# One product of 512 columns written as four of 128 in the recurrence of an RWKV-7 / forgetting-attention trunk

## The chip, the core and the metric

The kernel runs on one core of a Trainium2 chip. TensorE (PE) does matrix products, and the loading of its stationary operand is shown as an engine of its own (PEld). VectorE (DVE), ScalarE (ACT) and GpSimd (POOL) do the elementwise work, and SyncE (SP) issues most DMA transfers. The metric is the device time of one execution in microseconds (us). Before the change it is 2595.79 us, the median of three runs (2594.67 to 2596.96).

## The reference, cut to what matters

Two layers work on 256 tokens of width 2048 in float32: RWKV-7 time mixing with a SwiGLU, then forgetting attention with a SwiGLU. The change is in the first. Each of 32 heads of width 64 carries a 64x64 state through the tokens:

```python
def step(S, inp):
    r_t, w_t, k_t, v_t, a_t, b_t = inp
    sa = jnp.einsum('bhij,bhj->bhi', S, a_t)
    S = (S * w_t[:, :, None, :] + sa[..., None] * b_t[:, :, None, :]
         + v_t[..., None] * k_t[:, :, None, :])
    return S, jnp.einsum('bhij,bhj->bhi', S, r_t)
...
w_log = -jax.nn.softplus(-(w0 + jnp.tanh(xw @ w1) @ w2).astype(f32)) - 0.5
decay = jnp.exp(-jnp.exp(w_log))
```

The kernel does not step token by token. It works on chunks of 64 tokens and needs, for every token and channel, the product of the decays from the chunk's start, which is the exponential of a running sum of log decays.

## The kernel before, in words

**The weight stream.** Every large product runs in `Stream.gemm`: weights arrive by DMA in 128x1024 pieces (`st`), ACT rounds each 128x512 block to a high half (`wh`, L147), DVE subtracts to get the low half (`wl`, L148), and PE multiplies in three products of 512 columns each (L180 to L182). They are called large products here. They follow each other through the whole kernel.

**Background work.** After each group of three, `tick` lets up to eight generators go one step. They issue everything else, PE's small products included, so small products lie between the large ones in one queue on PE. The builder then places the instructions of every engine by its own estimate of when each is ready, so the final order differs in details from that of the code. Each engine executes its queue in order.

**The recurrence.** It is cut into eight units, one for each of four groups of eight heads and two halves of 128 tokens. For each unit four generators follow each other:
- `prepare` (L579) makes the decays and scaled keys. Its first product (L587) multiplies a constant 128x128 triangular matrix (two blocks of 64 tokens) with `tw`, the log decays of the unit: 128 tokens by 512 channels. The result fills one PSUM bank. DVE (L599) and two ACT exponentials (L600, L601) read the whole of it. Transposes (L642, L655, L669) and head products (L681, masked by DVE in L684) follow.
- `solve` (L695) copies diagonal blocks (L708, ACT) and inverts 8x8 triangles on DVE (L713 to L733).
- `merge` (L736) joins them with small 32x32 products (L758, L765, L775, L791), each run of which waits for DVE or ACT results (`Ti`, `Xs`).
- `chain` (L809) carries the state through the unit's two chunks (L838, L842, L848, L854, L856).
- `post` normalises the output, and transposes it (L911).

PE reads float32 operands of these small products as they are. In the trace such a product has two records of MATMUL and two of LDWEIGHTS, a transpose has one of each, and a large product, whose operands are rounded halves, one of each. The last unit's running sums are made at 489 us; the rest of the kernel, to 2597 us, has no instruction of the recurrence after about 590 us.

## Time and profile before

| | |
|---|---|
| median of 3 runs | 2595.79 us (2594.67 to 2596.96) |
| the profiled execution's own time | 2598.75 us |
| its span, first to last instruction | 2597.0 us |
| PE busy | 2549.0 us, 98% |
| DVE / ACT busy | 1694.3 us (65%) / 1409.5 us (54%) |
| chain that ended last, PE's share | 89% |
| the changed line, 8 products | 16 MATMUL records of 9.3 us in all |

Records on PE overlap: a record lasts from the product's start to its modelled end, and the next product starts before that. What a product costs is therefore read from the distance of starts, not from its duration. An idle time in square brackets at a row's end is time in which PE had nothing running, with what ended it.

### The profile page before, as it was taken

The numbers are of one execution on the slowest core, as the hardware profiler recorded it, in microseconds if no ns is written. First come the engines' busy times: TensorE is split into PE (matmuls) and PEld (weight loads), VectorE is DVE, ScalarE is ACT, GpSimd is POOL, SyncE is SP. The second block draws the span as 40 slices with busy tenths as digits, with TensorE's granted clock in tenths as the row PEclk, the third lists the DMA queues.
The fourth block names the chain that finished last, engine by engine and source line by source line (L and its number), as shares of the span: only waits on it lengthen the run. The fifth ranks groups of instructions, "written<-read, shape, count | busy, mean of one in ns | idle before, by whom it ended". The sixth has DMA issues, their size and how long they took to land.

```text
span 2597.0 us, 40783 instructions
## 1 busy us (share of the span) xinstructions
PE 2549.0 (98%) x15104; PEld 2081.7 (80%) x15104; DVE 1694.3 (65%) x3049; ACT 1409.5 (54%) x2605; POOL 90.1 (3%) x73
## 2 busy tenths in 40 slices
PE   7999999999999999999999999999999999999998
PEld 5788777778888888888888888888888888888887
DVE  7886999987555555555556777676655555555554
ACT  6665666556455544545545656555655545454444
POOL 0000011100000000000001011010000000000000
PEclk9999999999999999999999999999999999999999
DMA  6667434345565565555556666664565655565554
GB/s 193 183 201 241 135 102 115 110 140 186 188 193 187 189 192 186 192 189 188 193 191 204 191 210 181 187 203 152 190 194 186 189 189 189 187 193 188 194 195 162
DMA packets 271222, 472.66 MB, mean 182 GB/s; under 512 B 39464, under 2 KB 49976, under 8 KB 271024
## 3 DMA queue, kind: packets, MB, share of 16 engines
q1 hardware_dynamic: 267728, 467.33, 56.6%
q10 hardware_dynamic: 3136, 2.74, 0.3%
q8 instruction: 118, 1.93, 0.3%
q14 instruction: 80, 0.66, 0.1%
q0 software_dynamic: 160, 0.00, 0.0%
HBM read 459.47 MB, written 6.32 MB: 179 GB/s over the span
## 4 chain that ended last, share of the span: by engine, by line
PE 89%; DVE 5%; ACT 3%; DMA 2%; issue 1%; POOL 0%; SPq 0%; POOLq 0%; ACTq 0%; DVEq 0%
PE mm L180 27%; PE mm L181 27%; PE mm L182 27%; DVE wl L148 2%; ACT wh L147 1%; DMA st<-in_a_w_rkv_dram 1%; PE bg L1012 1%; PE bg L856 1%; PE bg L310 1%; PE bg L1248 0%; PE bg L838 0%; PE bg L848 0%; PE bg L462 0%; PE bg L854 0%; DMA x<-in_x_dram 0%
## 5 line engine op out<-in xcount | busy, mean ns | idle before, releaser
L148 DVE TENSOR_TENSOR wl<-st,wh 128x512 fp32r<-128x512 f32 (+1 forms) x1648 | 1128.1, 690 | 795.2 <-ACT wh L147 790.1
L147 ACT CAST wh<-st 128x512 fp32r<-128x512 f32 (+1 forms) x1648 | 1017.0, 622 | 980.0 <-DVE wl L148 688.5
L180 PE MATMUL mm<-wh,xb 128*128 128x512 f32 x2048 | 803.5, 392 | 0.0
L182 PE MATMUL mm<-wh,xb 128*128 128x512 f32 x2048 | 799.7, 390 | 0.0
L181 PE MATMUL mm<-wl,xb 128*128 128x512 f32 x2048 | 799.4, 390 | 0.0
L180 PEld LDWEIGHTS mm<-wh,xb 128*128 128x128 f32 x2048 | 384.7, 188 | 79.8 <-issue 3.3
L182 PEld LDWEIGHTS mm<-wh,xb 128*128 128x128 f32 x2048 | 384.5, 188 | 79.4
L181 PEld LDWEIGHTS mm<-wl,xb 128*128 128x128 f32 x2048 | 384.8, 188 | 75.8
L180 PE MATMUL mm<-wh,xa 128*128 128x512 f32 x768 | 310.3, 405 | 0.0
L181 PE MATMUL mm<-wl,xa 128*128 128x512 f32 x768 | 304.9, 397 | 1.5 <-DVE wl L148 1.5
L182 PE MATMUL mm<-wh,xa 128*128 128x512 f32 x768 | 304.3, 397 | 0.0
L180 PE MATMUL mm<-wh,hb 128*128 128x512 f32 x448 | 174.3, 389 | 0.0
L181 PE MATMUL mm<-wl,hb 128*128 128x512 f32 x448 | 174.3, 389 | 0.0
L182 PE MATMUL mm<-wh,hb 128*128 128x512 f32 x448 | 174.3, 389 | 0.0
L181 PEld LDWEIGHTS mm<-wl,xa 128*128 128x128 f32 x768 | 145.7, 190 | 30.8 <-DVE wl L148 3.2
L180 PEld LDWEIGHTS mm<-wh,xa 128*128 128x128 f32 x768 | 145.5, 190 | 31.0 <-issue 1.7
L182 PEld LDWEIGHTS mm<-wh,xa 128*128 128x128 f32 x768 | 145.2, 189 | 30.3
L181 PEld LDWEIGHTS mm<-wl,hb 128*128 128x128 f32 x448 | 84.1, 188 | 17.5
L180 PEld LDWEIGHTS mm<-wh,hb 128*128 128x128 f32 x448 | 84.1, 188 | 17.4
L182 PEld LDWEIGHTS mm<-wh,hb 128*128 128x128 f32 x448 | 84.1, 188 | 17.4
L1196 POOL TENSOR_TENSOR n<-n,pw 128x8 f32<-128x8 f32 x24 | 45.1, 1882 | 411.7 <-DVE n L1195 411.7
L1239 ACT ACTIVATE sc<-sc,nm 128x128 f32<-128x128 f32 x64 | 28.7, 449 | 26.6 <-DVE nm L1238 26.6
(294 smaller groups left out, 1826.2 us busy)
## 6 DMA issues: line engine op xcount, KB each, us to landing
st<-in_f_w_gu_dram SPq DMA_DIRECT2D x352, 512.0 KB
st<-in_f_w_d_dram SPq DMA_DIRECT2D x176, 512.0 KB
st<-in_b_w_in_dram SPq DMA_DIRECT2D x128, 512.0 KB
st<-in_a_w_rkv_dram SPq DMA_DIRECT2D x96, 512.0 KB
st<-in_a_w_o_dram SPq DMA_DIRECT2D x32, 512.0 KB
st<-in_b_w_o_dram SPq DMA_DIRECT2D x32, 512.0 KB
cb<-cdram SPq DMA_DIRECT2D x4, 1024.0 KB
x<-in_x_dram SPq DMA_DIRECT2D x12, 256.0 KB
```

Source lines behind the costliest of these rows:

```text
L147: nc.scalar.copy(hi[:rows, :n], st)
L148: nc.vector.tensor_tensor(lo[:rows, :n], st, hi[:rows, :n].bitcast(F32), op=ALU.subtract)
L180: nc.tensor.matmul(ps[t][:, :n], xh[:rows, c], wh, start=b == 0, stop=False)
L181: nc.tensor.matmul(ps[t][:, :n], xh[:rows, c], wl, start=False, stop=False)
L182: nc.tensor.matmul(ps[t][:, :n], xl[:rows, c], wh, start=False, stop=b == kts - 1)
L310: nc.tensor.transpose(tp[:, i * T + t * P : i * T + (t + 1) * P], src[:, t, c : c + P], ident)
L856: mm(pb[half[1 - q], ps_], M[:, q * 8 + s_, 0:C], vu[:, hs], start=first, stop=first or p == 3)
L1012: nc.tensor.transpose(tp[:, j * P : (j + 1) * P], h[:, j * P : (j + 1) * P], ident)
L1196: nc.gpsimd.tensor_tensor(n8[:, :], n8[:, :], pw[:, :], op=ALU.pow)
L1239: nc.scalar.activation(sc[:, c], sc[:, c], AF.Exp, bias=nm[:, t : t + 1], accum_out=nm[:, 2 + t : 3 + t])
```

## The change

The one product of 512 columns becomes four of 128 columns with the same stationary matrix. Each writes its quarter of the same PSUM bank, each with `start` and `stop` set. Nothing else is edited.

```diff
                     ps = yield from S.take()
-                    mm(ps[:, :], cst[:, C_TRI : C_TRI + P], tw[:, :], start=True, stop=True)
+                    for p in range(4):
+                        mm(ps[:, p * P : (p + 1) * P], cst[:, C_TRI : C_TRI + P], tw[:, p * P : (p + 1) * P], start=True, stop=True)
                     kk = u1.tile([P, 512], F32, name="kk")
                     nc.vector.tensor_tensor(kk[:, :], k, vk[:, :], op=ALU.mult)
```

The file gains a line, so lines from L588 on have a number that is one higher after the change (L758 becomes L759). Because the builder places instructions by its estimates, some others move too. On PE, at the first unit, the product stands where it stood. Before:

```order
L182 MATMUL mm<-wh,xa_1479 128x512
L587 MATMUL bg<-tw_2799,cst 128x512
L180 MATMUL mm<-wh,xa_1478 128x512
L181 MATMUL mm<-wl,xa_1478 128x512
L182 MATMUL mm<-wh,xa_1479 128x512
```

and after:

```order
L182 MATMUL mm<-wh,xa_1479 128x512
L588 MATMUL bg<-tw_2799,cst 128x128 x4
L180 MATMUL mm<-wh,xa_1478 128x512
L181 MATMUL mm<-wl,xa_1478 128x512
L182 MATMUL mm<-wh,xa_1479 128x512
```

Nothing moved here: four products stand in the place of one. The first difference in order on PE is behind the second unit's sums, at the first unit's merge (some 295 us into the span); `mm` are large products, `bg` small ones. Before:

```order
L180 MATMUL mm<-wh,xa_1478 128x512
L181 MATMUL mm<-wl,xa_1478 128x512
L758 MATMUL bg<-Ti,El 32x32 x32
L182 MATMUL mm<-wh,xa_1479 128x512
L180 MATMUL mm<-wh,xa_1478 128x512
L181 MATMUL mm<-wl,xa_1478 128x512
L765 MATMUL bg<-Xs,Tt 32x32 x32
L182 MATMUL mm<-wh,xa_1479 128x512
```

and after:

```order
L180 MATMUL mm<-wh,xa_1478 128x512
L759 MATMUL bg<-Ti,El 32x32 x32
L181 MATMUL mm<-wl,xa_1478 128x512
L182 MATMUL mm<-wh,xa_1479 128x512
L180 MATMUL mm<-wh,xa_1478 128x512
L766 MATMUL bg<-Xs,Tt 32x32 x32
L181 MATMUL mm<-wl,xa_1478 128x512
L182 MATMUL mm<-wh,xa_1479 128x512
```

Both runs of 32 small products stand one large product earlier, with three large products between them as before. The same happens in most places of the recurrence from here on where the order differs; in a few a run stands one later, and the five runs of the chain product L848 whose place differs go both ways. All 9888 large products stay, and the order is the same again behind the last unit.

On DVE, between the second unit's masks (L684) and its sums' first reader (L599), one instruction changes places with two. Before:

```order
L684 TENSOR_TENSOR xb_2580<-bg,cst 128x512 x2
L626 TENSOR_REDUCE bon<-rr 128x8
L684 TENSOR_TENSOR xb_2580<-bg,cst 128x512 x2
L631 TENSOR_TENSOR kk<-kk,n_3090 128x512
L148 TENSOR_TENSOR wl<-st,wh 97x512
L599 TENSOR_TENSOR WW<-bg,tw_2802 128x512
```

and after:

```order
L685 TENSOR_TENSOR xb_2580<-bg,cst 128x512 x2
L627 TENSOR_REDUCE bon<-rr 128x8
L632 TENSOR_TENSOR kk<-kk,n_3096 128x512
L685 TENSOR_TENSOR xb_2580<-bg,cst 128x512 x2
L148 TENSOR_TENSOR wl<-st,wh 97x512
L600 TENSOR_TENSOR WW<-bg,tw_2802 128x512
```

The scaling of the keys (`kk`) went ahead of the second pair of masks; what stands behind the two is unchanged up to the first unit's merge.

## Rows read from the trace of the kernel before

**Rows 1.** The page: busy time of each engine, and the share of each engine in the chain of work that ended last.

```profile
PE 2549.0 (98%) x15104; PEld 2081.7 (80%) x15104; DVE 1694.3 (65%) x3049; ACT 1409.5 (54%) x2605; POOL 90.1 (3%) x73
...
PE 89%; DVE 5%; ACT 3%; DMA 2%; issue 1%; POOL 0%; SPq 0%; POOLq 0%; ACTq 0%; DVEq 0%
```

**Rows 2.** Busy time by stage: before the recurrence, the recurrence, and the rest. [...]

```profile
0.00:256.00 256.00, 233.02 (x1088) 190.91 (x1089) 198.45 (x412) 154.43 (x317) 5.48 (x11) 0.99 0.66 204
256.00:584.00 328.00, 311.84 (x4789) 238.53 (x4788) 296.52 (x673) 202.40 (x425) 33.57 (x28) 0.99 0.41 122
584.00:2597.00 2013.00, 2004.10 (x9231) 1652.26 (x9229) 1199.36 (x1966) 1052.71 (x1863) 51.09 (x34) 1.00 0.59 189
```

**Rows 3.** The line that changes, L587: durations in ns (least, median, most), first and last start, shape; then what its readers waited for it (us, times).

```profile
L587 PEld LDWEIGHTS bg<-tw,cst x16: 186/188/189, 260.2 to 488.7; 128*128 128x128 f32 x16
L587 PE MATMUL bg<-tw,cst x16: 590/592/1061, 260.4 to 489.2; 128*128 128x512 f32 x16
...
  DVE WW L599: 0.4, 1
```

**Rows 4.** PE in order of time around the second of the eight products (start us, duration us, instruction).

```profile
281.27 1.02 PE L587 MATMUL bg<-tw,cst 128*128 128x512 f32 x2
281.72 0.80 PE L180 MATMUL mm<-wh,xa 128*128 128x512 f32 x1
282.36 0.40 PE L181 MATMUL mm<-wl,xa 128*128 128x512 f32 x1
282.59 0.39 PE L182 MATMUL mm<-wh,xa 128*128 128x512 f32 x1
```

**Rows 5.** PE in order of time where float32 products of 64 columns, each with a new 128x128 stationary operand, follow each other (in the attention layer).

```profile
1463.95 0.39 PE L1256 MATMUL bg<-v,pT 128*128 128x64 f32 x2
1464.17 0.39 PE L1257 MATMUL bg<-v,pT 128*128 128x64 f32 x2
1464.40 0.39 PE L1255 MATMUL bg<-v,pT 128*128 128x64 f32 x2
```

**Rows 6.** PE in order of time around eight transposes of 128 columns, each with a 128x128 stationary operand.

```profile
474.76 1.09 PE L655 MATMUL bg<-cst,WW 128*128 128x128 f32 x8
475.61 0.71 PE L182 MATMUL mm<-wh,xa 128*128 128x512 f32 x2
476.16 0.40 PE L180 MATMUL mm<-wh,xa 128*128 128x512 f32 x1
476.40 0.39 PE L181 MATMUL mm<-wl,xa 128*128 128x512 f32 x1
```

**Rows 7.** In order of time, PE and DVE around the longest idle time of PE in the recurrence, the first unit's merge.

```profile
294.67 0.39 PE L181 MATMUL mm<-wl,xa 128*128 128x512 f32 x1
...
298.04 0.63 DVE L732 STREAM_TRANSPOSE Ti<-Xb 128x256 f32<-128x256 f32 x1
...
298.77 1.07 PE L758 MATMUL bg<-Ti,El 32*32 32x32 f32 x64 [3.72 <-issue]
```

**Rows 8.** Stretches of 2 us from there on, and one later in the recurrence; columns as in rows 2.

```profile
296.00:298.00 2.00, 0.00 (x0) 0.00 (x0) 1.95 (x5) 0.14 (x1) 0.14 (x1) 1.00 0.00 0
298.00:300.00 2.00, 1.23 (x65) 1.19 (x66) 2.00 (x6) 0.11 (x1) 0.22 (x1) 0.71 0.00 0
300.00:302.00 2.00, 2.00 (x51) 1.25 (x55) 1.98 (x4) 0.85 (x2) 0.00 (x0) 0.50 0.42 100
302.00:304.00 2.00, 2.00 (x98) 1.50 (x92) 1.47 (x5) 0.66 (x2) 0.00 (x0) 0.94 0.70 238
...
408.00:410.00 2.00, 2.00 (x24) 0.60 (x25) 2.00 (x4) 1.93 (x5) 0.00 (x0) 0.52 0.53 202
```

**Rows 9.** PE in order of time at three more idle times in the recurrence.

```profile
399.40 0.52 PE L758 MATMUL bg<-Ti,El 32*32 32x32 f32 x37 [0.69 <-DVE Ti L767]
...
451.37 0.68 PE L848 MATMUL bg<-u,TT 64*64 64x64 f32 x16 [0.77 <-ACT u L846]
...
515.12 0.38 PE L758 MATMUL bg<-Ti,El 32*32 32x32 f32 x21 [2.02 <-issue]
```

**Rows 10.** What PE waited for most between 258 and 600 us (who, for whom; us in total, times, longest).

```profile
PE bg L758 <- issue: 6.0, 3, 3.7
PE bg L848 <- ACT u L846: 3.8, 5, 1.2
PE bg L765 <- issue: 1.7, 3, 1.0
PE bg L758 <- DVE Ti L767: 1.5, 3, 0.7
PE bg L669 <- DVE xb L659: 1.1, 4, 0.4
```

**Rows 11.** DVE and ACT in order of time between the second unit's masks and sums.

```profile
282.21 1.27 DVE L684 TENSOR_TENSOR xb<-bg,cst 128x512 f32<-128x512 f32 x2
283.40 0.68 DVE L631 TENSOR_TENSOR kk<-kk,n 128x512 f32<-128x512 f32 x1
...
283.87 1.23 ACT L708 COPY Dg<-xb 32x256 f32<-32x256 f32 x3
...
285.20 0.41 DVE L713 TENSOR_TENSOR Xb<-Dg,cst 128x256 f32<-128x256 f32 x1
```

## The prediction

> **What bounds the kernel now.** I read the page's busy times and its chain first [rows 1]. PE is busy for 98% of the span and holds 89% of the chain that ended last; DVE has 5%, ACT 3%. Next comes the table by stage [rows 2], since an average over the span hides where PE is not alone. From 584 us on PE is busy for 2004.10 of 2013 us. In the recurrence, 256 to 584 us, it is busy for 311.84 of 328 us: 16.2 us idle, while DVE is busy for 296.52 us, 90% of the stretch. So in the changed stage PE's own time is the first limit, and DVE's chains are the second. What PE waits for there is in the list of waits [rows 10]: merge products and state products, waiting for DVE and ACT. No row of that list names the changed line, and its readers waited for it once, for 0.4 us [rows 3].

> Two things can therefore change the time: what PE needs for four products in place of one, and what the changed order does to PE's idle time.

> **The products themselves.** L587 has 16 records for 8 products, so each product is two passes over its 512 columns [rows 3]. In order of time [rows 4], L587 starts at 281.27; the next large product is queued from 281.72 and the one behind it starts at 282.36. Large products follow each other in 0.23 us (282.36 to 282.59), so the queued one had its turn at 282.13. L587 thus takes 282.13 - 281.27 = 0.86 us, 0.43 a pass. That is 0.1075 us for 128 columns. Four products need eight passes of 128 columns: streamed without a gap, again 0.86 us. The low end is no change; a gain is excluded, since the same columns pass at the same pace.

> What is new is that the stationary matrix is loaded eight times per unit, not twice. The trace has no float32 product of 128 columns with a new full stationary operand, so I bound it by neighbours. With 64 columns and a new 128x128 operand [rows 5], a product starts every 0.2225 us (1463.95, 1464.17, 1464.40), 0.111 a pass. Streaming 64 columns takes 0.054, so something else sets that pace, and only the load is there. Either it runs beside the stream and takes 0.111 itself; then a pass of 128 columns takes 0.111, eight take 0.89, and a unit costs 0.03 more: 0.2 us over eight units. Or it stands in series and takes 0.111 - 0.054 = 0.057; then a pass takes 0.165, eight take 1.32, and a unit costs 0.46 more: 3.7 us. The nearest row in shape is eight transposes, of 128 columns and with 128x128 operands [rows 6]: they start at 474.76; the third large product behind them starts at 476.16, which puts the end of the eight at 476.16 - 2 x 0.23 = 475.70. That is 0.94 for eight, 0.1175 each. I take this one: 0.08 us more a unit, **0.6 us** over eight.

> [...]

> **The changed order.** The builder gives four products other estimates than one, so runs of small products move against the large ones, mostly one place ahead. At the first unit's merge, PE is idle for 3.72 us until L758 starts at 298.77, when DVE's L732 (298.04 plus 0.63) is done [rows 7]. DVE works through those microseconds without a gap [rows 8], so L732 does not come sooner or later. L758 now stands one large product earlier: PE waits 0.23 longer and runs that product afterwards, where PE has no idle time and the granted clock is 0.50 [rows 8]. That is 2 x 0.23 = 0.46 us. At 399.40 [rows 9] L758 waits for L767, which depends on L765; four large products stand between these as before, and both move together: nothing. At 451.37 [rows 9] L848 waited 0.77 for ACT and stands one large product later: 0.23 less. At 515.12 [rows 9] nothing moves. The sum is **0.2 us**. Where a moved run meets no idle time, the same work is done in another order, at no cost.

> On DVE the second pair of masks starts 0.60 later (282.81 for 282.21). The ACT copies behind them (L708) ended at 283.87 + 1.23 = 285.10 and L713 took them at 285.20 [rows 11]. Now the second mask ends near 284.1 and two copies of 0.41 end near 284.9: covered by L599, and if it were not, at most 0.6 us. On SP, some loads of the state's values change places with one weight load; PE waits for ACT and DVE in rows 10, for no DMA, so I cost that at nothing; without this cover a late piece would cost PE what it is late.

> The bounds of the order as a whole are wide. Some 27 runs stand one large product earlier; if all met idle time, it would be 27 x 0.23 = 6.2 us more. Downwards, the idle time of rows 10, 14.1 us in five rows, could in part go. The places that I could follow say 0.2, and I stay there.

> **Sum.** The profiled execution took 2598.75 us, 1.75 more than its span. 2598.75 + 0.6 + 0.2 = 2599.6. That execution is 2.96 us (0.11%) above the median of the runs, so for the median I say 2595.79 + 0.8 = **2596.6 us**. A measurement of this kernel tells a change from none at about 0.2%, here 5.2 us: 2590.6 to 2601.0 is no change.

> **Rivals.**
> - *The loads stand in series with the streams* (0.165 a pass): 3.7 + 0.2, or 2599.7 us, still no change. Were the whole 0.111 load and nothing hidden, a pass would take 0.111 + 0.1075 = 0.2185, a unit 1.75, and the kernel 7.1 us more: 2603.1 us, slower. For it: nothing in these rows hides a float32 load behind a float32 stream of 128 columns beyond doubt. Against it: rows 6 at 0.1175. [...] 5% for the smaller, 2% for the larger.
> - *A new long wait and a drop of the clock*: slower. Behind the 3.72 us of idling the granted clock was 0.71, 0.50 and 0.94 in three stretches of 2 us [rows 8], which loses 0.58 + 1.00 + 0.12 = 1.7 us. A second place like it costs 3.7 + 1.7 = 5.4, with the 0.8 above 6.2: 2602.0 us. The clock falls at a second place now, near 408 us [rows 8]; a third could be the merge at 515.12, which idles 2.02 already [rows 9]; DVE is 90% busy, so a step of solve put behind two others is late by more than one of them. It decides from about 4.4 us of added loss on. Against it: the exchanges on DVE are by one or two places. 6%.
> - *The long wait at 298.77 shrinks or another goes*: faster. If the 3.72 and the 1.7 behind it went, 0.8 - 5.4 = -4.6: 2591.2 us, short of the bound alone; with 0.77 from 451.37 it is 2590.4. Against it: L732 ends a chain of DVE that has no gap. 4%.

> **Chances and range.** The forecast holds 83%, the series rival 5% of no change, the larger 2%, the new wait 6%, the lost wait 4%. Faster 0.04, same 0.88, slower 0.08. The unknown of the order sets the range: about 3.5 us down; up by 3.7 for the series price and a little: 2593.0 to 2601.0.

> **What would show it.** L588 has 64 MATMUL and 64 LDWEIGHTS records; starts inside a group of eight lie 0.11 to 0.12 apart, where 0.165 shows the series and 0.21 the larger price. PE's idle time from 256 to 584 us stays within 3 us of 16.2; L759 still starts near 298.8 behind some 3.95 us of idling; the clock falls there and near 408 us and at no third place; the stage behind keeps its length. A recurrence that is longer by over 4 us with PE no busier would prove me wrong by the order, and one with PE busier by as much, by the loads.

## The result, and the profile after

The changed kernel takes 2600.14 us, the median of 22 runs (2594.37 to 2607.64), against 2595.82 of the kernel before (22 runs, 2594.03 to 2600.73): the ratio is 1.0015, with a 95% interval of 1.001 to 1.0021. That is no change by the bound of 0.2% and inside the range (2593.0 to 2601.0). It is also 4.3 us, clear of zero, where the forecast had 0.8. The cause of that difference is what the experiments are about.

The page of the changed kernel answers to [rows 1]; PE has 48 more records, as 64 stand for 16:

```profile
PE 2549.7 (98%) x15152; PEld 2087.4 (80%) x15152; DVE 1694.0 (65%) x3049; ACT 1410.2 (54%) x2605; POOL 89.5 (3%) x73
...
q8 instruction: 119, 1.95, 0.3%
...
PE 90%; DVE 4%; DMA 2%; ACT 2%; issue 1%; SPq 0%; POOLq 0%; POOL 0%; ACTq 0%; DVEq 0%
```

The row in the middle is from the list of DMA queues: packets, MB, share of 16 engines. 119 packets of 1.95 MB are 16 KB each; it matters below.

PE in order of time around the second unit's four products, to be read against [rows 4], and the line's durations, against [rows 3]:

```profile
277.66 0.40 PE L182 MATMUL mm<-wh,xa 128*128 128x512 f32 x1
277.90 1.05 PE L588 MATMUL bg<-tw,cst 128*128 128x128 f32 x8
278.70 0.48 PE L180 MATMUL mm<-wh,xa 128*128 128x512 f32 x1
279.02 0.39 PE L181 MATMUL mm<-wl,xa 128*128 128x512 f32 x1
...
L588 PE MATMUL bg<-tw,cst x64: 271/275/377, 257.0 to 493.5; 128*128 128x128 f32 x64
```

By the same working as before, the eight passes end where the next large product had its turn, 279.02 - 0.23 = 278.79, and took 278.79 - 277.90 = 0.89 us, 0.111 each. That fits the load running beside the stream, at the pace of [rows 5]; in series it would have been 0.165 or more. On PEld the eight loads start at 277.76 and their records last 0.99 us in all, so they lie beside the eight passes in time. One product of 512 columns took 0.86, so four cost 0.03 more a unit, 0.24 us in eight units. In five of the eight units one of the seven distances between starts is 0.213 in place of 0.111. That is not a price of the change: the kernel before has the same 0.105 more between its two passes there (0.533 for 0.428), in four of the five units, and in the fifth its product ran at the lower clock.

By stage the difference is in the recurrence. The rows are to be read against [rows 2]; the columns there and here are the stretch and its length, busy us of PE, PEld, DVE, ACT and POOL, each with its instructions, the granted clock of PE as a share of its full one, the DMA share, GB/s:

```profile
256.00:584.00 328.00, 310.65 (x4814) 242.73 (x4814) 292.71 (x667) 198.59 (x419) 32.94 (x28) 0.97 0.40 118
584.00:2598.00 2014.00, 2005.33 (x9238) 1653.83 (x9236) 1200.78 (x1968) 1054.20 (x1865) 51.08 (x34) 1.00 0.62 189
```

The granted clock over the stretch is 0.97 where it was 0.99. The two spans differ by 0.9 us only, because the profiled execution of before had lost time earlier. From 60 to 100 us its granted clock was 0.91, against 1.00 after; before and after:

```profile
60.00:100.00 40.00, 36.99 (x172) 29.99 (x172) 35.25 (x79) 24.45 (x53) 0.00 (x0) 0.91 0.61 179
```

```profile
60.00:100.00 40.00, 37.83 (x189) 30.52 (x188) 36.91 (x83) 26.89 (x59) 0.00 (x0) 1.00 0.61 186
```

That costs 40 x 0.09 = 3.6 us, ahead of the first changed instruction. So I compare the recurrence alone, from the first record of the running sums to the last of the outputs' transposes (L911, after the change L912). Before it is 585.6 - 260.4 = 325.2 us [first start in rows 3; the last start of L911 is 585.6]. After it is 587.3 - 257.0 = 330.3. The recurrence grew by 5.1 us in this pair of profiles.

Where PE stood idle in it, to be read against [rows 7] and [rows 9]:

```profile
295.38 1.08 PE L759 MATMUL bg<-Ti,El 32*32 32x32 f32 x64 [3.87 <-issue]
...
431.65 0.74 PE L759 MATMUL bg<-Ti,El 32*32 32x32 f32 x62
435.03 0.26 PE L759 MATMUL bg<-Ti,El 32*32 32x32 f32 x2 [2.65 <-issue]
...
470.01 0.65 PE L766 MATMUL bg<-Xs,Tt 32*32 32x32 f32 x52
472.04 0.31 PE L766 MATMUL bg<-Xs,Tt 32*32 32x32 f32 x12 [1.38 <-issue]
```

The first is the forecast wait, 3.87 us. The others are of another kind. A run of 32 equal products (64 records) is stopped after 62 records, or after 52, although the run had already been released. Behind both stops the granted clock falls to its lower level, 0.50:

```profile
434.00:436.00 2.00, 0.97 (x6) 0.88 (x6) 0.45 (x2) 0.37 (x1) 0.00 (x0) 0.73 0.12 33
436.00:438.00 2.00, 2.00 (x57) 1.67 (x59) 1.92 (x6) 1.16 (x3) 0.00 (x0) 0.50 0.03 8
...
472.00:474.00 2.00, 1.96 (x25) 1.17 (x26) 1.55 (x5) 0.00 (x0) 0.00 (x0) 0.62 0.65 193
474.00:476.00 2.00, 2.00 (x33) 1.74 (x30) 2.00 (x5) 1.16 (x3) 0.00 (x0) 0.50 0.78 237
476.00:478.00 2.00, 2.00 (x6) 1.39 (x5) 1.02 (x4) 1.92 (x6) 0.84 (x1) 0.50 0.28 103
478.00:480.00 2.00, 2.00 (x39) 1.51 (x38) 1.46 (x3) 1.60 (x4) 0.80 (x1) 0.68 0.00 0
```

Summed over stretches of 2 us from 250 to 592 us, (1 - clock) times the stretch is 3.4 us before and 8.5 us after; PE's idle time is 16.2 and 17.4 us. So the recurrence grew mostly by work done at the lower clock. Of the 5.1 us more, 1.7 stand at the first merge and 1.7 + 3.4 behind the two stops, and the 1.7 near 408 us of before [rows 8] are gone.

### The profile page after: what moved, and what is told of

The parts are those of the page before. It is cut to its first block, busy times and chain, and to the rows that moved or that the text cites. A ratio compares the mean times of both kernels' runs of the same rounds, so it can differ in the third digit from the quotient of the medians.

```text
span 2597.9 us, 40880 instructions
## 1 busy us (share of the span) xinstructions
PE 2549.7 (98%) x15152; PEld 2087.4 (80%) x15152; DVE 1694.0 (65%) x3049; ACT 1410.2 (54%) x2605; POOL 89.5 (3%) x73
## 3 DMA queue, kind: packets, MB, share of 16 engines
q8 instruction: 119, 1.95, 0.3%
## 4 chain that ended last, share of the span: by engine, by line
PE 90%; DVE 4%; DMA 2%; ACT 2%; issue 1%; SPq 0%; POOLq 0%; POOL 0%; ACTq 0%; DVEq 0%
PE mm L180 28%; PE mm L181 27%; PE mm L182 27%; DMA st<-in_a_w_rkv_dram 1%; DVE wl L148 1%; PE bg L1013 1%; PE bg L857 1%; PE bg L310 1%; ACT wh L147 0%; PE bg L839 0%; PE bg L1249 0%; PE bg L849 0%; PE bg L855 0%; DVE xmf L375 0%; DMA st<-in_a_w_o_dram 0%
## 5 line engine op out<-in xcount | busy, mean ns | idle before, releaser
L180 PEld LDWEIGHTS mm<-wh,hb 128*128 128x128 f32 x448 | 84.1, 188 | 17.4
L181 PEld LDWEIGHTS mm<-wl,hb 128*128 128x128 f32 x448 | 84.1, 188 | 17.4
```

The costliest lines, as they stand in the source:

```text
L180: nc.tensor.matmul(ps[t][:, :n], xh[:rows, c], wh, start=b == 0, stop=False)
L181: nc.tensor.matmul(ps[t][:, :n], xh[:rows, c], wl, start=False, stop=False)
```

## What stops a run in its middle

The kernel before has such stops as well: the run at 515.12 in [rows 9] had done 43 of 64 records. I counted the position of each stop in PE's program, with a LDWEIGHTS and a MATMUL for each record and the few instructions that only wait. In the profile of before the six stops inside a run stand at instruction 6337, 6594, 7617, 9922, 10945 and 11201; in that of after the three stand at 7617, 8897 and 9922. All nine leave 193 or 194 when divided by 256. PE has 30384 such instructions in the trace of before and 30482 in that of after, and 256 go into them 118.7 and 119.1 times: the page's queue q8, "instruction", has 118 and 119 packets of 16 KB. Its 1.93 and 1.95 MB come to 63.6 and 64.0 bytes for each of those instructions, and 16 KB over 256 to 64.

To forecast with it I worked out a count, an estimate: over all borders of the recurrence, how much less than 4.5 us the 256 instructions before a border take, by distances of starts (0.2275 us for a large product, 0.1175 for a transpose, 0.0107 for a 32x32 record, and so on). It is 15.7 us before and 19.6 after. Only its differences mean something, since its size hangs on the 4.5 us, a choice that no run measures. It stands in the expectations of the last four runs below and not in those of the first two, whose times were known by then: for these two it is no forecast.

**The packets in time.** The trace has a start and a duration for each packet of that queue, so the theory can be tested without any new run. Taken in order there is one packet for each border, from the second border on. The packet for the stop at 435.03 is alone in its queue in a stretch of a quarter of a microsecond (432.50 to 432.75 us):

```profile
q8 instruction: 1, 0.02, 23.8%
```

23.8% of 16 engines in 0.25 us is 0.95 us. By the trace it starts at 432.61, so it has landed at 433.56, and PE goes on 1.47 us later. For the stop at 472.04 it is 469.57 + 1.19 = 470.76, 1.28 us earlier. The same holds in all profiles of this case: the six stops of before, the three of after and the 13 of five runs below end 1.24 to 1.56 us after their packet has landed. None of the borders in the eight profiles, stop or not, is passed sooner than 1.24 us after its packet's landing. The packets start between 5.0 us before and 4.7 us after PE passes the border one piece earlier. So a piece that is used up faster than the next one starts, lands and is taken over ends in a stop.

The stops at borders add up to 4.4 us in the profile of before, in six, and to 4.4 us in that of after, in three. So it is not their sum that differs between these two profiles, but the time at the lower clock.

## Experiments

The ratios below are those on record, each with its 95% interval; they are not quotients of the medians.

**Borders moved, order kept.** Extra products of 8 columns at the very start, where PE waits for its input (11.3 us for the DMA of `gr` in the profile of before), write into a free part of a tile that nobody reads. Everything else on PE keeps its order.

```diff
             tp = now(S.take())
+            for _ in range(18): mm(tp[0:8, 256:264], pw[:, 0:8], pw[:, 0:8], start=True, stop=True)
             nc.tensor.transpose(tp[:, 0:112], gr[0:112, 0, :], ident[0:112, 0:112])
```

In the kernel before:

> The kernel before with 18 extra products of 8 columns (72 PE instructions) at the very start, where PE waits for its first input; their result is read by nobody, and the order of everything else on PE is that of before. Fetch theory (PE's instructions arrive in pieces of 256, and where the border between two pieces falls into a run of short products PE waits for the next piece): the borders move by 72 instructions, into denser runs, so slower than before by 3 to 6 us, 2599 to 2602 us, with idle times inside runs of the 32x32 products that are not there before. Order theory (the moved runs of small products cost the time): no change, 2595.8 within 1.5 us, since the order is that of before. Product theory (four products of 128 columns cost more than one of 512): no change, since the product is that of before.

Measured: 2598.51 us against 2596.11 of the kernel before in the runs beside it, ratio 1.0006 (0.9997 to 1.0015). The time is just under the range I gave, a miss of the fetch theory's size, and its interval includes no change, so by itself it decides nothing. Its profile does say where the borders went:

```profile
432.81 0.24 PE L759 MATMUL bg<-Ti,El 32*32 32x32 f32 x2 [1.57 <-issue]
...
470.08 0.25 PE L766 MATMUL bg<-Xs,Tt 32*32 32x32 f32 x5 [1.32 <-issue]
...
516.23 0.25 PE L766 MATMUL bg<-Xs,Tt 32*32 32x32 f32 x3 [0.62 <-issue]
```

They come behind 62, 59 and 61 of the 64 records, at instructions 7618, 8898 and 10178, which leave 194 again. In the kernel before none of the three stood there.

In the changed kernel:

> The changed kernel with the same 18 extra products of 8 columns at the start, where PE waits; the order of the rest is that of the changed kernel. Fetch theory: the borders move into sparser places than in the changed kernel, and sparser than in the kernel before, so 4 to 6 us less than the changed kernel, 2594 to 2597 us, at or below the kernel before. Order theory and product theory: as the changed kernel, 2600 us within 1.5, since order and products are the same.

Measured: 2593.93 us (2590.98 to 2597.77), ratio to the kernel before 0.9992 (0.9983 to 1.0001). This is 6.2 us less than the changed kernel takes, though PE's order and its products are unchanged and more was added. Order theory and product theory fall here. Its recurrence lasts 579.9 - 255.8 = 324.1 us, and the two places where the clock fell after the change show it undisturbed, with small stops only:

```profile
364.75 0.44 PE L760 MATMUL bg<-Ti,El 32*32 32x32 f32 x27 [0.24 <-issue]
...
432.20 0.53 PE L760 MATMUL bg<-Ti,El 32*32 32x32 f32 x38 [0.70 <-issue]
...
434.00:436.00 2.00, 1.68 (x70) 1.22 (x62) 1.90 (x5) 1.49 (x4) 0.00 (x0) 1.00 0.12 27
472.00:474.00 2.00, 2.00 (x14) 1.80 (x15) 1.65 (x5) 1.94 (x4) 1.12 (x1) 1.00 0.50 183
```

**Is it the extra work at the start that helps?** The same edit with 64 products, one whole piece, and with 50:

```diff
+            for _ in range(64): mm(tp[0:8, 256:264], pw[:, 0:8], pw[:, 0:8], start=True, stop=True)
```

> The changed kernel with 64 extra products of 8 columns at the start, 256 PE instructions: one whole piece. Fetch theory: the borders fall on the same instructions as in the changed kernel, so as slow as that, 2600 us within 2, and the idle times stand inside the same runs of 32x32 products. If instead extra products at the start help by themselves (a busier PE while it waits for its input, an earlier first stage), 64 of them help no less than 18 did: 2594 us or less.

Measured: 2599.56 us (2597.53 to 2600.89), ratio 1.0013 (1.0004 to 1.0022). A whole piece gives the changed kernel's time back, and its stops, after the same records (62 and 52):

```profile
435.48 0.26 PE L760 MATMUL bg<-Ti,El 32*32 32x32 f32 x2 [3.07 <-issue]
...
473.91 0.31 PE L767 MATMUL bg<-Xs,Tt 32*32 32x32 f32 x12 [1.06 <-issue]
```

> The changed kernel with 50 extra products of 8 columns at the start, 200 PE instructions. Fetch theory: counted over the borders, the time by which the 256 instructions before a border take less than 4.5 us is 14.3 us, as with 18 extra products (14.4) and below the changed kernel's 19.6: 2594 us within 2. If the gain grows with the number of extra products or is chance, it has no reason to come back here: 2600 us, or somewhere between.

Measured: 2594.45 us (2592.61 to 2596.91), ratio 0.9998 (0.9989 to 1.0007). So 0, 18, 50 and 64 extra products give 2600.1, 2593.9, 2594.5 and 2599.6 us: the time goes with the position within a piece, not with how much is added.

**The count without the products of 128 columns.**

```diff
                     ps = yield from S.take()
+                    for _ in range(3):
+                        mm(ps[0:8, 0:8], pw[:, 0:8], pw[:, 0:8], start=True, stop=True)
                     mm(ps[:, :], cst[:, C_TRI : C_TRI + P], tw[:, :], start=True, stop=True)
```

> The kernel before, its one product of 512 columns kept, with three extra products of 8 columns ahead of it in each unit, so that the number of PE instructions per unit is that of the changed kernel. Fetch theory: the borders move as in the changed kernel (20.8 us by the count above, 19.6 there), so 2599 to 2603 us though no product of 128 columns is there. Product theory: 2596 to 2597 us, since three products of 8 columns in eight units cost PE some 1 us.

Measured: 2600.74 us (2597.48 to 2603.39), ratio 1.0015 (1.0006 to 1.0024): the loss of the changed kernel, with its number of instructions and without its products. In its profile a unit's three small products start about 0.026 us a record apart (six records in 0.30 us, the last of 0.169), 0.16 us for the six, or 1.3 us in eight units, where the forecast of the product theory had some 1 us. The order on PE differs from both kernels here, so this run alone does not part order from borders; the runs above do. Its profile also has a fall of the clock, from 373.87 us, behind a wait for DVE that ends at 373.06 (0.99 us). This one stands at a border too, but its packet had landed 6.75 us earlier, so it is no wait for instructions.

**Two products of 256 columns.**

```diff
-                    mm(ps[:, :], cst[:, C_TRI : C_TRI + P], tw[:, :], start=True, stop=True)
+                    for p in range(2):
+                        mm(ps[:, p * 256 : (p + 1) * 256], cst[:, C_TRI : C_TRI + P], tw[:, p * 256 : (p + 1) * 256], start=True, stop=True)
```

> Two products of 256 columns in place of the four of 128: four more PE instructions per unit than before, not twelve. Fetch theory: 14.8 us by the count above, a little below the kernel before (15.7), so 2594 to 2597 us. Product theory: between the two kernels, 2597 to 2598 us, since the number of products and loads lies between.

Measured: 2594.76 us (2590.88 to 2595.34), ratio 0.9995 (0.9986 to 1.0004). In products and loads it lies between the two kernels, in time it does not.

Together, with the recurrence of each profile (first sum to last output transpose), and from 250 to 592 us the time lost by the clock, PE's idle time and, of it, the stops at borders that the profile puts down to "issue":

| kernel | count, us | median, us | recurrence, us | lost by clock | PE idle | stops |
|---|---|---|---|---|---|---|
| changed + 50 | 14.3 | 2594.45 | 324.3 | 5.1 | 14.5 | 1.7 |
| changed + 18 | 14.4 | 2593.93 | 324.1 | 3.4 | 15.0 | 0.9 |
| two of 256 | 14.8 | 2594.76 | 325.9 | 5.1 | 16.7 | 3.2 |
| before | 15.7 | 2595.82 | 325.2 | 3.4 | 16.2 | 4.4 |
| changed | 19.6 | 2600.14 | 330.3 | 8.5 | 17.4 | 4.4 |
| changed + 64 | 19.6 | 2599.56 | 330.0 | 6.8 | 19.1 | 4.9 |
| 512 and three small | 20.8 | 2600.74 | 330.9 | 6.8 | 17.4 | 3.5 |
| before + 18 | 21.0 | 2598.51 | 327.3 | 6.8 | 17.0 | 3.5 |

The count parts the versions into those at 14 to 16 us, with medians of 2593.9 to 2595.8 us, and those at 19 to 21, with 2598.5 to 2600.7 us. Within a group it does not give the order, and the kernel before with 18 has the highest count and the least time of its group. The last four columns are of one profiled execution each, and the granted clock differs between executions of one kernel (0.992 to 0.998 over the changed kernel's 22 runs), so a single row there says less than a median. Stops alone do not order the times either. Of the nine stops longer than 1.3 us, seven have a fall of the clock that begins before the stop ends or within 1.5 us of its end; the two without are that at 515.12 us before and one of 1.37 us at 474.63 us with three small products.

No version beats the kernel before beyond doubt: the best, the changed kernel with 18 extra products, has an interval up to 1.0001. Its median is 6.2 us below that of the changed kernel.

## Why the prediction was right, and where it was off

- **The products** were forecast at 0.6 us, from the transposes' 0.1175 a pass. A pass takes 0.111, and eight units cost 0.24 us by the unit worked out above. The value to take was the one from [rows 5], the same kind of product; the series reading (0.165) is out, and so is the larger price (0.2185, an estimate with the whole 0.111 as load and nothing hidden). By the 0.111, the eight loads of the 128x128 matrix ran beside the passes: at the pace of the 512-column product 128 columns take 0.1075, so some 0.004 us a pass was not hidden.
- **The wait at the first merge** was forecast at 3.95 us and was 3.87, and L759's run still ends the idle time when DVE is done. The low clock behind it lasted longer in this execution (3.4 us lost in place of 1.7), which I had not forecast. The changed kernel with 18 and with 50 extra products lose the same 3.4 there, so it is not what parts the versions.
- **"The same work is done in another order, at no cost"** is the step that failed. The order costs nothing that these runs can show, as the changed kernel with 18 extra products has it and is no slower than the kernel before. What was left out is the position of the work in PE's instruction stream, a term that the sum put at nothing: the median moved by 4.3 us where the forecast had 0.8, and it came back to 2593.93 us when 72 instructions moved the borders.
- **The rival of a new long wait with a drop of the clock** had the right shape and the wrong cause. Two new stops came, at 435.03 and 472.04, both with a fall of the clock. It is not a late step of DVE, and not the place that I named. The stop at 515.12 was misread: the bracket says "issue", and the row begins with 21 records of a run of 64. A run whose first 43 records have gone is not waiting for its data, and its packet landed at 513.73, 1.39 us before it went on. The list in [rows 10] was misread in the same way, as waits for DVE and ACT: 1.7 us at L765 and 2.3 of the 6.0 us at L758 are "issue" at borders, 4.0 of the 14.1 us.
- **The clock** "at no third place" was wrong: of the two places, the one near 408 us is gone in this execution, and two others came.
- **The signs** named for being wrong misled. The recurrence grew by 5.1 us, and PE's busy time in it from 325.2 - 16.2 = 309.0 to 330.3 - 17.4 = 312.9 us, which was to speak for the loads. It is the same work at the lower clock.
- **The sum** missed by 3.5 us for that missing term. The range, made wide for the unknown of the order and the series price, held the time for a reason that it was not made for: that it held is luck.

What stays open: the profile does not name the instructions that a packet carries; that a stop is a wait for its piece rests on the positions, the packets' size and order, their landings and the runs above. How long a stop is (0.2 to 3.1 us in these profiles) follows from when its packet lands; what sets a packet's start, and why a long stop is not always followed by a fall of the clock, was not resolved, nor was a kernel tried without any border in a dense run.

## What to carry to other kernels

Here an edit that added 96 instructions to PE, busy for 98% of the span, moved all code behind it against the borders of PE's pieces of 256. In a stage with runs of 64 records at 0.0107 us a record, that weighed more than the edit itself: 0.24 us of work, and some 4 us of borders with the granted clock of 0.50 behind them. Another kernel may show the same where a busy engine runs many very short instructions; that was not tried. Before a few us are put down to an edit, try it with another number of idle instructions ahead of it, and once with a whole piece. And read in an idle row how much of its run has gone: a stop in the middle of equal instructions, put down to "issue", may be no wait for data; look then when the packets of the instruction queue landed.

## What the runs showed of the hardware that was not expected

- The nine stops inside a run in the two kernels' profiles all stand at 193 or 194 modulo 256 of PE's instructions, and in the two runs of 18 extra products, in that of 50 and of 64, and in that of two products of 256 columns, all 13 leave the same 193 or 194. In the run with three small products the four stops put down to "issue" do so as well.
- In all eight profiles PE passes no border sooner than 1.24 us after the landing of that piece's packet of 16 KB, and the 22 stops end 1.24 to 1.56 us after it.
- 72 extra instructions at the start of the program, where PE waits for its input, moved the changed kernel's time by 6.2 us, by what happens some 400 us later, and 256 moved it by 0.6, within its spread.
- A stop of 1.38 us inside a dense run was followed by four stretches of 2 us at 0.62, 0.50, 0.50 and 0.68 of the clock, while a stop of 2.02 us in the profile of before was followed by none.
